# Softmax weights divided by their sums before the transposes, instead of the product after them

## The chip, the core and the metric

One core of a Trainium2 chip (trn2) runs the whole program. Its engines run side by side, each its own instructions in order: TensorE (PE in the rows, PEld for its weight loads), VectorE (DVE), ScalarE (ACT), GpSimd (POOL), and SyncE (SP), which here only issues transfers. They wait for one another by semaphores. The metric is the device time of one execution in microseconds; lower is better.

## The reference, cut to what matters

One layer of a streaming encoder, for 512 prompt frames and 64 sample frames with a cache of 128: a projection, two kinds of attention with 8 heads each, an output projection, two layer norms and a feed-forward part. The change concerns the last lines of both attentions, the softmax and the product with the values:

```
def fox_attend(q, k, v, cum_q, cum_k, q_pos, k_pos):
    s = jnp.einsum('bqhd,blhd->bhql', q, k, ...) * HEAD_DIM ** -0.5
    decay = cum_q[..., None] - cum_k[..., None, :]
    p = jax.nn.softmax(jnp.where(mask, s + decay, NEG), axis=-1)
    return jnp.einsum('bhql,blhd->bqhd', p.astype(v.dtype), v)

def dsa_attend(...):
    ...
    s = jnp.einsum('bqhd,bqkhd->bhqk', q, kg, ...) * HEAD_DIM ** -0.5
    p = jax.nn.softmax(jnp.where(valid[:, None], s, NEG), axis=-1)
    return jnp.einsum('bhqk,bqkhd->bqhd', p.astype(vg.dtype), vg)
```

`dsa_attend` keeps for each frame only the keys of the highest index scores. The division by the sum of a row may be done to the weights p, or to the product with v: both give the same result.

## The kernel before

Features lie on the partitions, the 576 frames (512 and 64) along the free axis. Products of full precision are made of three products of split numbers (a high part that ACT casts, a low part that DVE or POOL subtracts), in `gemm`, L279, 288 columns at a time. Weights come by DMA into a ring of raw buffers, ACT casts the high half (L183), DVE or POOL subtracts the low half (L187).

The heads go in eight **pairs** (p = 0 to 7): pairs 0 to 3 are the forgetting attention, 4 to 7 the indexed one. While the attention of pair p runs, the projection of pair p+1 (`proj`) runs between its steps: `drive` gives out the projection in groups of six products and puts a step of the attention between groups. Beside pair 7 runs the first part of the output projection (`wo1`).

A pair has nine **jobs**: a block of 128 query frames i = 0 to 3 for each of two heads hh (so 128, 256, 384 or 512 keys), and one job s for the 64 sample frames of both heads. A **tick** starts one job, and `PLAN` says which stage of which earlier job is due in this tick: (stage, lag) means that the stage is applied to the job started lag ticks ago. A tick has three groups of stages, with one group of projection products between two groups, and takes some 3 us. The stages of before:

- `qk`, lag 0: scores into a PSUM tile S (L825, L827; L818 for the job s)
- `addmax`, lag 1: DVE adds the bias (`causal`, `dbias`, `biasS`, `dbiasS`) and finds the row's extreme (L835), into an SBUF tile `sP`
- `exp`, lag 2: ACT takes the exponential in place (L843) and adds up each row; the sums of the eight prompt jobs go to a tile `sums` of the pair
- `norm`, lag 2: for the job s alone: DVE inverts its own sum (L848), ACT multiplies the weights (L849); then DVE inverts the pair's `sums` (L851) and ACT spreads them over 512 columns, `rows` (L853)
- `ptrans`, lag 3: PE transposes the weights in blocks of 128x128 into a PSUM tile T (the helper of all transposes is L65)
- `pevac`, lag 3: T goes to SBUF, by ACT for pairs 0 to 3 (L891), by DVE for 4 to 7 (L893)
- `scales`, lag 3: PE transposes `rows`, four blocks, into a PSUM tile X
- `pv`, lag 4: 24 products of weights and values into the PSUM tile V (L913) once a pair; two for the job s into a tile X (L902, L903)
- `oevac`, lag 5: once a pair, ACT copies the job s (L923) and the transposed sums (L924) to `mix32`, DVE multiplies V by them (L925), ACT casts the high part BH (L926), POOL subtracts the low part BL (L927).

The tiles S, T and X share one ring of three PSUM banks (tag R, `psum_1`): a fourth tile waits for the reader of the first. V has a bank of its own. The big projection tiles m have two buffers.

Beside the first pair (some 54 to 86 us) the index scores are made: PE makes a head's logits (L608), ACT takes the relu (L613) into one of four slices of `work`, DVE adds them up in `dbias` (L616, L618). They use the same three PSUM banks. Then DVE chooses the highest scores in rounds of MAX8 and MATCH_REPLACE8 (L642, L644), until some 189 us, in between its other work. Tiles named `st` hold the extremes and sums of a job and the eight maxima of a round.

The order of the instructions on each engine is fixed when the program is built.

Of the kernel before, what the change touches and what calls it, by code (L numbers as in the profile page):

```python
# [8 lines left out]
F32 = mybir.dt.float32  # L9
F32R = mybir.dt.float32r  # L10
AF = mybir.ActivationFunctionType
OP = mybir.AluOpType
# [3 lines left out]
NT = 576  # L16
NP = 512
# [19 lines left out]
def tile_hybrid_step(ctx: ExitStack, tc: tile.TileContext, I, O):  # L37
    nc = tc.nc
    PE, ACT, DVE, POOL, SP = nc.tensor, nc.scalar, nc.vector, nc.gpsimd, nc.sync
# [4 lines left out]
    def f(ap):  # L44
        return ap.bitcast(F32)
# [18 lines left out]
    def transpose(out, in_, n):  # L64
        PE.transpose(out, in_, ident[:n, :n])  # L65
# [23 lines left out]
    def drive(main, n_main, bg, n_bg, drain=True, close=True):  # L89
        done = 0  # L90
        for i, _ in enumerate(main):
            clock[0] += 1
            pop_due(POP)
            for fl in fillers:
                fl()
            while bg is not None and done * n_main < (i + 1) * n_bg:
                done += 1
                if next(bg, 0) == 0:
                    bg = None
                    break  # L100
        if close:
            flush()
        if bg is not None and drain:
            for _ in bg:
                pass
# [181 lines left out]
    sb = pA.enter_context(tc.tile_pool(name="sb", bufs=1))  # L287
# [7 lines left out]
    def psum_1(tag, bufs, dt=F32):  # L295
        return psA.tile([128, 512], dt, name=tag, tag="V" if tag == "V" else "R", bufs=1 if tag == "V" else 3)
# [369 lines left out]
    pair = {0: {}}  # L666
# [134 lines left out]
    BH = BL = None  # L801
# [27 lines left out]

    def addmax(j):  # L830
        n = j["S"].shape[1]
        t = sb.tile([128, 512], F32, name="sP", bufs=4)
        st = stats()
        j["P"], j["st"] = t[:, :n], st
        DVE.tensor_tensor_reduce(j["P"], j["S"], j["bias"], scale=1.0, scalar=-GONE, op0=OP.add, op1=OP.min,  # L835
                                 accum_out=st[:, 0:1])

    def exp(j):
        P = pair[j["p"]]
        if "sums" not in P:  # L840
            P["sums"] = sb.tile([128, 2, 4], F32, name="sums", bufs=2)
        s = j["st"][:, 2:3] if j["s"] else P["sums"][:, j["hh"], j["i"]:j["i"] + 1]
        ACT.activation(j["P"], j["P"], AF.Exp, bias=j["st"][:, 0:1], scale=-1.0, accum_out=s)  # L843

    def norm(j):

        if j["s"]:
            DVE.reciprocal(j["st"][:, 3:4], j["st"][:, 2:3])  # L848
            ACT.mul(j["P"], j["P"], j["st"][:, 3:4])  # L849
            sums = pair[j["p"]]["sums"]  # L850
            DVE.reciprocal(sums, sums)  # L851
            rows = pair[j["p"]]["rows"] = sb.tile([128, 4, 2, 64], F32, name="rows", tag="tok", bufs=2)
            ACT.copy(rows, sums.rearrange("p h (i o) -> p i h o", o=1).to_broadcast([128, 4, 2, 64]))  # L853

    def scales(j):

        if not j["s"]:
            return
        rows = pair[j["p"]]["rows"]
        ps = j["R"] = psum_1("X", 1)  # L860
        for i in range(4):
            transpose(ps[:, i * 128:i * 128 + 128], rows[:, i].rearrange("p h c -> p (h c)"), 128)

    def ptrans(j):
        ps = psum_1("T", 1)
# [50 lines left out]
    def oevac(j):  # L916
        if not j["s"]:
            return
        p = j["p"]
        mx = sb.tile([128, NT], F32, name="mix32", tag="mix32")  # L920
        for hh in range(2):
            r = slice(hh * 64, hh * 64 + 64)
            ACT.copy(mx[r, NP:], j["O"][r, r])  # L923
        ACT.copy(mx[:, :NP], j["R"])  # L924
        DVE.tensor_tensor(mx[:, :NP], pair[p]["O"], mx[:, :NP], OP.mult)  # L925
        ACT.copy(BH[:, p], mx)  # L926
        POOL.tensor_tensor(BL[:, p], mx, f(BH[:, p]), OP.subtract)  # L927

    def jobs_of(p):
        out = [dict(p=p, hh=hh, i=i, s=False, close=i % 2 == 1 and hh == 1) for i in range(4) for hh in range(2)]  # L930
        return out + [dict(p=p, s=True, close=True)]

    PLAN = (((oevac, 5), (addmax, 1), (exp, 2), (make_bias, 0), (make_bias, -1)),
            ((ptrans, 3), (norm, 2)),
            ((qk, 0), (pevac, 3), (scales, 3), (pv, 4)))

    all_jobs = [j for p in range(8) for j in jobs_of(p)]
    tick_no = [0]
# [72 lines left out]
    for p in range(7):  # L1011
        if p == 1:
# [3 lines left out]
            BH = base.tile([128, 8, NT], F32R, name="BH", tag="BH")  # L1016
# [24 lines left out]
    def wo1():  # L1041
        side = delayed(1, v_out(7))
        for j in range(8):
            u = U["o", j]
            W = WT.use(u)
            WT.ahead(u + 1)
            m = psum_m()
            for h in range(2):
                if (j, h) == (7, 1):
                    WT.ahead(u + 2)  # L1050
                for _ in gemm(m[:, h, :HW], W, range(6), BH, BL, slice(h * HW, (h + 1) * HW)):
                    WT.step()
                    if j == 0:
                        next(side, 0)
                    yield 1
                if j in (5, 6) and h == 0:
                    p_split(j - 5)
            y = Y[:, j].rearrange("p (a c) -> p a c", a=2)
            later(0, lambda y=y, m=m: DVE.scalar_tensor_tensor(
                y, y, ALPHA, m[:, :, :HW], op0=OP.mult, op1=OP.add))  # L1060

    drive(wo1(), 48, ticks(9 + 5), 42)
    pPA.close()
    pA.close()

# [488 lines left out]
```

## Time and profile before

| | |
|---|---|
| median of three runs | 781.4 us (781.35, 782.94, 781.4) |
| profiled execution | 782.97 us |
| its span, first to last instruction | 781.2 us |
| PE busy | 771.7 us, 99% |
| DVE busy | 554.7 us, 71% |
| ACT busy | 441.1 us, 56% |
| POOL busy | 118.9 us, 15% |
| TensorE clock granted | 1.000 |

Busy time is that of instructions at work; the rest of the span is waiting. In the rows of the profile a duration of a matmul is its time from issue to end, and matmuls overlap: what one costs the queue is read from the chain of waits, or from the distance between two starts. Rows of the chain and of the timeline begin with the start and the length in us; "x4" means four instructions merged in the row; what stands in brackets is the idle time before, and what ended it. Rows of the waits give the total, the number and the longest.

### The profile page before, as it was taken

To read this page: it belongs to the slowest core of one execution; us is meant where nothing else is said; L and a number is where in the kernel's file an instruction comes from. 1 tells how busy PE (TensorE), PEld (TensorE's weight loads), DVE (VectorE), ACT (ScalarE), POOL (GpSimd) and SP (SyncE) were. 2 spreads that over 40 slices of the span, in tenths; PEclk is the share of its full clock that TensorE was granted. 3 is DMA by queue.
4 is the path that set the end of the run, shared out by engine and by line. 5 is a ranking of instruction groups with operands and counts; after the bars stand their busy time and mean duration, and the time that the engine had idled before them with its cause. 6 is when DMAs were issued, how large, how long until landed. Compare 5 with 4: busy or idle time off the path is not lost.

```text
span 781.2 us, 14772 instructions
## 1 busy us (share of the span) xinstructions
PE 771.7 (99%) x5798; PEld 755.1 (97%) x5798; DVE 554.7 (71%) x1124; ACT 441.1 (56%) x924; POOL 118.9 (15%) x121
## 2 busy tenths in 40 slices
PE   9999999999999999999999999999999999999997
PEld 8988899999999999999999999999999999999997
DVE  7578787897556555989988666677666686557553
ACT  5468766788777644587366434444434454526351
POOL 8102345354332000110000000000000000022200
PEclk9999999999999999999999999999999999999999
DMA  8627233253323233441143222323222313630001
GB/s 298 204 37 173 66 113 107 88 181 115 111 65 92 73 96 112 143 164 56 55 135 108 84 79 83 109 84 105 78 63 103 110 55 112 231 130 28 28 28 67
DMA packets 31125, 81.43 MB, mean 104 GB/s; under 512 B 5072, under 2 KB 10192, under 8 KB 30928
## 3 DMA queue, kind: packets, MB, share of 16 engines
q1 hardware_dynamic: 30768, 80.27, 33.1%
q8 instruction: 45, 0.74, 0.4%
q14 instruction: 24, 0.20, 0.1%
q10 hardware_dynamic: 288, 0.22, 0.1%
HBM read 66.38 MB, written 9.54 MB: 97 GB/s over the span
## 4 chain that ended last, share of the span: by engine, by line
PE 90%; DVE 5%; ACT 2%; issue 1%; DMA 1%; POOL 0%; DVEq 0%; ACTq 0%; SPq 0%
PE g L279 54%; PE m L279 20%; PE n L279 3%; PE V L913 2%; PE T L65 2%; PE S L827 1%; PE X L65 1%; PE S L825 1%; DVE dbias L618 1%; PE m L419 1%; PE m L426 1%; PE S L426 1%; DVE whl L187 1%; DMA wraw<-in_w_up_dram 0%; DMA iraw<-in_w_idx_dram 0%
## 5 line engine op out<-in xcount | busy, mean ns | idle before, releaser
L183 ACT CAST whl<-wraw 128x512 fp32r<-128x512 f32 (+1 forms) x228 | 137.4, 611 | 179.8 <-PE g L279 150.5
L187 DVE TENSOR_TENSOR whl<-wraw,whl 128x512 fp32r<-128x512 f32 (+1 forms) x194 | 132.5, 694 | 79.0 <-ACT whl L183 78.6
L279 PE MATMUL m<-AH,whl 128*128 128x288 f32 x736 | 177.7, 308 | 0.0
L279 PE MATMUL g<-BH,whl 128*128 128x288 f32 (+2 forms) x784 | 162.9, 296 | 0.5 <-DVE Y L1219 0.5
L279 PEld LDWEIGHTS g<-BH,whl 128*128 128x128 f32 x784 | 127.7, 188 | 1.2 <-DVE Y L1219 1.0
L279 PEld LDWEIGHTS m<-AH,whl 128*128 128x128 f32 x736 | 126.3, 188 | 1.9 <-issue 1.0
L279 PE MATMUL g<-BL,whl 128*128 128x288 f32 (+2 forms) x392 | 115.5, 295 | 0.0
L279 PE MATMUL m<-AL,whl 128*128 128x288 f32 x368 | 109.0, 296 | 0.0
L279 PE MATMUL g<-hidO,whl 128*128 128x288 f32 (+2 forms) x768 | 103.8, 295 | 0.0
L279 PE MATMUL g<-hidE,whl 128*128 128x288 f32 (+2 forms) x768 | 103.7, 295 | 0.0
L279 PEld LDWEIGHTS g<-hidO,whl 128*128 128x128 f32 x768 | 102.5, 188 | 0.0
L279 PEld LDWEIGHTS g<-hidE,whl 128*128 128x128 f32 x768 | 102.2, 188 | 0.1
L279 PEld LDWEIGHTS g<-BL,whl 128*128 128x128 f32 x392 | 73.8, 188 | 0.2
L279 PE MATMUL g<-s,whl 128*128 128x288 f32 x504 | 71.3, 295 | 0.0
L279 PEld LDWEIGHTS m<-AL,whl 128*128 128x128 f32 x368 | 69.5, 189 | 0.7
L279 PEld LDWEIGHTS g<-s,whl 128*128 128x128 f32 x504 | 68.2, 188 | 0.0
L1109 POOL TENSOR_TENSOR ln_s<-Y 128x576 f32<-128x576 f32 (+2 forms) x3 | 4.4, 1468 | 374.5 <-DVE Y L1386 362.1
L187 POOL TENSOR_TENSOR whl<-wraw,whl 128x512 fp32r<-128x512 f32 x34 | 44.5, 1308 | 75.1 <-ACT whl L183 57.5
L843 ACT ACTIVATE sP<-sP,st 128x128 f32<-128x128 f32 (+4 forms) x72 | 39.6, 550 | 25.3 <-DVE st L835 24.9
L279 PE MATMUL m<-BH,whl 128*128 128x288 f32 x192 | 43.4, 304 | 0.0
L1362 DVE TENSOR_TENSOR Y<-Y,g 128x576 f32<-128x576 f32 x40 | 30.0, 749 | 14.5 <-PE g L279 14.5
L279 PEld LDWEIGHTS m<-BH,whl 128*128 128x128 f32 x192 | 32.1, 188 | 0.4 <-issue 0.3
(280 smaller groups left out, 1278.0 us busy)
## 6 DMA issues: line engine op xcount, KB each, us to landing
wraw<-in_w_up_dram SPq DMA_DIRECT2D x32, 512.0 KB, 3.5
wraw<-in_w_down_dram SPq DMA_DIRECT2D x32, 512.0 KB, 3.4
wraw<-in_w_qkv_dram SPq DMA_DIRECT2D x23, 512.0 KB, 3.8
wraw<-in_w_gate_dram SPq DMA_DIRECT2D x8, 512.0 KB, 4.0
wraw<-in_w_o_dram SPq DMA_DIRECT2D x8, 384.0 KB, 3.1
out_vT_dram<-v SPq DMA_DIRECT2D x8, 288.0 KB, 2.1
Y<-in_xT_dram SPq DMA_DIRECT2D x8, 288.0 KB, 4.7
PLD<-PL SPq DMA_DIRECT2D x4, 576.0 KB, 3.5
```

Of the source, the lines that this page charges most:

```text
L65: PE.transpose(out, in_, ident[:n, :n])
L183: ACT.copy(self.hv[h][0], src)
L187: eng.tensor_tensor(lv, src, f(hv), OP.subtract)
L279: PE.matmul(ps, W(w, kw, wc), a[:, ka, cols], start=(first and i == 0), stop=(last and i == n - 1))
L419: PE.matmul(mk[:, h, :HW], w0(part, k), a[:, k, h * HW:(h + 1) * HW], start=(k == 0 and i == 0), stop=(k == 7 and i == 2))
L426: PE.matmul(acc[b][:n[b], :304], a[:, k, b * 128:b * 128 + n[b]], ixw(part, k), start=(k == 0 and i == 0), stop=(k == 7 and i == 2))
L618: DVE.scalar_tensor_tensor(dst[:n, :nk], r[:n, :nk], w, dst[:n, :nk], op0=OP.mult, op1=OP.add)
L825: PE.matmul(ps[:, :n], Q[:, c], K[:, :n], start=True, stop=False)
L827: PE.matmul(ps[:, :n], Q[:, c], P["KL"][:, hh, :n], start=False, stop=True)
L843: ACT.activation(j["P"], j["P"], AF.Exp, bias=j["st"][:, 0:1], scale=-1.0, accum_out=s)
L913: PE.matmul(P["O"][r, (i - 1) * 128 + c.start:(i + 1) * 128], P["vt"][:, kb, r], t[:, hh, kb, c], start=(kb == 0), stop=(kb == i))
L1362: later(0, lambda y=y, m=m: DVE.tensor_tensor(y, y, m[:, :, :HW], OP.add))
```

## The change

Each job's weights are now divided by their sum, before the transposes: `norm` inverts the sum of every job on DVE (L843 of the changed file), and multiplies its weights on ACT (L845), for the first pair on POOL (L847). The pair's `sums`, `rows` and the stage `scales` are gone, and with them 32 transposes. `oevac` writes BH straight from PSUM with ACT (L910) and BL with DVE (L911), for V and for the two parts of the job s; `mix32` and POOL's subtraction are gone. `ptrans` and `pevac` have lag 4, `pv` 5, `oevac` 6, the tiles `sP` five buffers, and the attention 45 steps beside `wo1` instead of 42.

```
     def addmax(j):
-        t = sb.tile([128, 512], F32, name="sP", bufs=4)
+        t = sb.tile([128, 512], F32, name="sP", bufs=5)
...
     def exp(j):
-        P = pair[j["p"]]
-        if "sums" not in P:
-            P["sums"] = sb.tile([128, 2, 4], F32, name="sums", bufs=2)
-        s = j["st"][:, 2:3] if j["s"] else P["sums"][:, j["hh"], j["i"]:j["i"] + 1]
-        ACT.activation(j["P"], j["P"], AF.Exp, bias=j["st"][:, 0:1], scale=-1.0, accum_out=s)
+        ACT.activation(j["P"], j["P"], AF.Exp, bias=j["st"][:, 0:1], scale=-1.0, accum_out=j["st"][:, 2:3])
 
     def norm(j):
-        if j["s"]:
-            DVE.reciprocal(j["st"][:, 3:4], j["st"][:, 2:3])
+        DVE.reciprocal(j["st"][:, 3:4], j["st"][:, 2:3])
+        if j["p"]:
             ACT.mul(j["P"], j["P"], j["st"][:, 3:4])
-            sums = pair[j["p"]]["sums"]
-            DVE.reciprocal(sums, sums)
-            rows = pair[j["p"]]["rows"] = sb.tile([128, 4, 2, 64], F32, name="rows", tag="tok", bufs=2)
-            ACT.copy(rows, sums.rearrange("p h (i o) -> p i h o", o=1).to_broadcast([128, 4, 2, 64]))
-
-    def scales(j):
-        if not j["s"]:
-            return
-        rows = pair[j["p"]]["rows"]
-        ps = j["R"] = psum_1("X", 1)
-        for i in range(4):
-            transpose(ps[:, i * 128:i * 128 + 128], rows[:, i].rearrange("p h c -> p (h c)"), 128)
+        else:
+            POOL.tensor_scalar(j["P"], j["P"], j["st"][:, 3:4], None, op0=OP.mult)
...
     def oevac(j):
-        mx = sb.tile([128, NT], F32, name="mix32", tag="mix32")
+        parts = [(BH[:, p, :NP], BL[:, p, :NP], pair[p]["O"])]
         for hh in range(2):
             r = slice(hh * 64, hh * 64 + 64)
-            ACT.copy(mx[r, NP:], j["O"][r, r])
-        ACT.copy(mx[:, :NP], j["R"])
-        DVE.tensor_tensor(mx[:, :NP], pair[p]["O"], mx[:, :NP], OP.mult)
-        ACT.copy(BH[:, p], mx)
-        POOL.tensor_tensor(BL[:, p], mx, f(BH[:, p]), OP.subtract)
+            parts.append((BH[r, p, NP:], BL[r, p, NP:], j["O"][r, r]))
+        for hi, lo, ps in parts:
+            ACT.copy(hi, ps)
+            DVE.tensor_tensor(lo, ps, f(hi), OP.subtract)
...
-    PLAN = (((oevac, 5), (addmax, 1), (exp, 2), (make_bias, 0), (make_bias, -1)),
-            ((ptrans, 3), (norm, 2)),
-            ((qk, 0), (pevac, 3), (scales, 3), (pv, 4)))
+    PLAN = (((oevac, 6), (addmax, 1), (exp, 2), (make_bias, 0), (make_bias, -1)),
+            ((ptrans, 4), (norm, 2)),
+            ((qk, 0), (pevac, 4), (pv, 5)))
...
-    drive(wo1(), 48, ticks(9 + 5), 42)
+    drive(wo1(), 48, ticks(9 + 6), 45)
```

What this does to the order of the instructions, at three places.

TensorE, at the end of the first pair, where its value products stood (X of `rows` are the four transposes of the sums, V the value products):

```order
 L825 MATMUL S<-kE,qE 128x256
 L827 MATMUL S<-KLP_150,fox 128x256
-L65 MATMUL X<-ident,rows 128x128 x4
-L913 MATMUL V<-PT,vtok 64x256 x2
-L913 MATMUL V<-PT,vtok 64x128 x2
-L913 MATMUL V<-PT,vtok 64x256 x6
-L913 MATMUL V<-PT,vtok 64x128 x2
```

and one job of the next pair further on:

```order
 L825 MATMUL S<-kO,qO 128x256
 L827 MATMUL S<-KLP_150,fox 128x256
-L902 MATMUL X<-PTs,Vc 128x128
-L903 MATMUL X<-PTs,VS_157 128x128
+L898 MATMUL V<-PT,vtok 64x256 x2
+L898 MATMUL V<-PT,vtok 64x128 x2
+L898 MATMUL V<-PT,vtok 64x256 x6
+L898 MATMUL V<-PT,vtok 64x128 x2
```

The transposes of the sums have left the queue, and the value products stand one job later, where the job s had its own, which follow a job later again.

ScalarE, near the end of the index logits beside the first pair. Before:

```order
L843 ACTIVATE sP,sums<-sP,st 128x512
L613 ACTIVATE work<-S 64x192
L853 COPY rows<-sums 128x512
L613 ACTIVATE work<-X 64x192
L891 COPY PT<-T 128x3x128
L685 COPY v_1149<-m 128x576
```

and now:

```order
L839 ACTIVATE sP,st<-sP,st 128x512
L613 ACTIVATE work<-S 64x192
L613 ACTIVATE work<-X 64x192
L876 COPY PT<-T 128x3x128
L685 COPY v_1157<-m 128x576
```

The copy that spreads the sums, and that waits for DVE's inverse of them, stood between two relus of logits; nothing stands there now. The work of this pair's `norm` went to POOL, whose queue over the same stretch is now:

```order
L847 TENSOR_SCALAR sP<-sP,st 128x256 x2
L187 TENSOR_TENSOR whl<-wraw,whl 128x512
L847 TENSOR_SCALAR sP<-sP,st 128x384
L711 CAST fox<-qs 64x512
L712 CAST fox<-qs 64x512
L187 TENSOR_TENSOR whl<-wraw,whl 128x512
L847 TENSOR_SCALAR sP<-sP,st 128x384
L847 TENSOR_SCALAR sP<-sP,st 128x512
L187 TENSOR_TENSOR whl<-wraw,whl 128x512
L847 TENSOR_SCALAR sP<-sP,st 128x512
```

The multiplications (L847) are new; the casts and the weight halves between them stood there before.

VectorE, beside pair 3, between the additions of the bias of its last prompt job and of its job s. Before:

```order
L835 ISA sP,st<-S,causal 128x512
L835 ISA st 128x1
L728 TENSOR_TENSOR qE<-x_2248,qE 64x576
L729 TENSOR_TENSOR qO<-x_2248,qO 64x576
L642 MAX st<-dbias_99 128x8
L851 RECIPROCAL sums<-sums 128x8
L644 MATCH_REPLACE dbias_99<-st,dbias_99 128x512
L642 MAX st<-dbias_99 128x8
L835 ISA sP,st<-S,biasS 128x192
```

and now:

```order
L835 ISA sP,st<-S,causal 128x512
L835 ISA st 128x1
L728 TENSOR_TENSOR qE<-x_2269,qE 64x576
L729 TENSOR_TENSOR qO<-x_2269,qO 64x576
L642 MAX st<-dbias_99 128x8
L843 RECIPROCAL st<-st 128x1 x2
L644 MATCH_REPLACE dbias_99<-st,dbias_99 128x512
L642 MAX st<-dbias_99 128x8
L835 ISA sP,st<-S,biasS 128x192
```

The rounds of the choice stand as they did; the inverse of the pair's sums has become the inverses of two single jobs, each behind ACT's exponential of its job.

## The prediction, made before the changed kernel ran

> **What bounds the kernel now.** First the page: busy time of each engine, then the busy time of stretches, one a pair or more.
>
> ```profile
> PE 771.7 (99%) x5798; PEld 755.1 (97%) x5798; DVE 554.7 (71%) x1124; ACT 441.1 (56%) x924; POOL 118.9 (15%) x121
> 66.00:94.00 28.00, 26.41 (x186) 24.16 (x184) 23.36 (x59) 21.29 (x60) 8.97 (x8) 1.00 0.44 129
> 122.40:150.75 28.35, 28.35 (x224) 27.26 (x225) 22.53 (x65) 19.45 (x51) 14.16 (x13) 1.00 0.37 108
> 150.75:179.10 28.35, 28.35 (x223) 27.22 (x224) 25.20 (x63) 24.01 (x58) 13.59 (x11) 1.00 0.52 163
> 179.10:207.40 28.30, 28.30 (x224) 27.21 (x223) 18.22 (x57) 22.75 (x53) 11.79 (x9) 1.00 0.30 97
> 345.00:700.00 355.00, 355.00 (x2697) 354.95 (x2696) 259.70 (x434) 171.20 (x289) 2.59 (x2) 1.00 0.31 100
> ```
>
> The columns of a stretch are its length, then PE, PEld, DVE, ACT and POOL busy with their instructions, the clock and the DMA share. TensorE is busy without a gap in the middle pairs, and from 345 to 700 us, behind the attention: what leaves its queue there shortens the run, as long as nothing it waits for gets late. Only beside the first pair does it miss 1.59 us of 28. The waits say for whom:
>
> ```profile
> PE X L608 <- ACT work L613: 1.4, 2, 1.2
> PE g L279 <- DVE Y L1219: 0.5, 1, 0.5
> ```
>
> So the first pair is bound by ACT and DVE, which make the index logits, and the rest by TensorE. Beside pair 3 (the fourth row) DVE is at 89% and ACT at 85%: that is where added work could show.
>
> **The change: what leaves TensorE.** The chain of waits gives the pace, here of the end of the first pair:
>
> ```profile
> 93.52 0.12 PE S L827
> 93.64 0.44 PE X L65 x4
> 94.08 2.31 PE V L913 x24
> ```
>
> ```profile
> L65 PE MATMUL X<-ident,rows 128*128 128x128 f32 x32 | 4.8, 272 | 0.0
> ```
>
> Four transposes hold the queue for 0.44 us, 0.11 each; 32 of them make 3.5 us. The value products (2.31 us a pair), the transposes of the weights and those of the job s stay, a tick later; the step of the plan adds no product. By the group's mean of 272 ns they would make 8.7 us; but that is the time from issue to end of one that overlaps its neighbours, and the queue moved on after 0.11. I take 3.5 us. The Trainium skill (TensorE: Matmul & The Clock Gate, Part 4: PE-mode transpose) gives about 275 ns for such a transpose inside a kernel, so it would come to some 8.8 us; the 272 ns agree with its figure, the 0.44 us for four don't agree with that use of it.
>
> **What is added to ACT and DVE in pairs 1 to 7.** These rows price it:
>
> ```profile
> L843 ACT ACTIVATE sP<-sP,st 128x512 f32<-128x512 f32 x16 | 11.5, 719 | 7.7 <-DVE st L835 7.6
> L843 ACT ACTIVATE sP<-sP,st 128x384 f32<-128x384 f32 x16 | 9.9, 616 | 6.3 <-DVE st L835 6.2
> L843 ACT ACTIVATE sP<-sP,st 128x256 f32<-128x256 f32 x16 | 8.2, 510 | 0.2
> L843 ACT ACTIVATE sP<-sP,st 128x128 f32<-128x128 f32 x16 | 6.4, 401 | 10.5 <-DVE st L835 10.5
> L849 ACT ACTIVATE sP<-sP,st 128x192 f32<-128x192 f32 x8 | 3.7, 457 | 0.2 <-DVE st L848 0.2
> L853 ACT COPY rows<-sums 128x512 f32<-128x512 f32 x8 | 4.9, 614 | 0.9 <-DVE sums L851 0.9
> L926 ACT CAST BH<-mix 128x576 fp32r<-128x576 f32 x8 | 5.4, 669 | 0.1
> L848 DVE RECIPROCAL st<-st 128x1 f32<-128x1 f32 x8 | 1.3, 161 | 1.1 <-ACT sP L843 0.9
> L851 DVE RECIPROCAL sums<-sums 128x8 f32<-128x8 f32 x8 | 1.6, 198 | 2.2 <-ACT sP L843 2.1
> ```
>
> The multiplication of the job s took as long as its exponential (0.457 us), so the eight others get the exponentials' durations: 2 x (0.401 + 0.510 + 0.616 + 0.719) = 4.5 us of ACT a pair. `rows` (0.614) and the cast of `mix32` (0.669) go; the copy of the transposed sums becomes the cast of V, 512 columns either way. ACT gains some 3.2 us a pair. DVE gains eight inverses of 0.161 less one of 0.198, 1.1 us; its multiplication by the sums becomes the subtraction of V, the same size; two subtractions of 64x64 are new, which no row shows. Bounded by the inverse of a single column (0.161) and by the addition of the bias over 192 columns (0.34, in a row below), they get 0.2 each, near the smaller one. DVE gains 1.5 us a pair, POOL loses a subtraction.
>
> What covers this? The weights must be divided before their transposes, and these come a tick later, some 3 us. In the tightest place that I looked at:
>
> ```profile
> 158.48 0.51 ACT L843 ACTIVATE sP<-sP,st 128x256 f32<-128x256 f32 x1
> 162.09 0.38 PE L65 MATMUL T<-ident,sP 128*128 128x128 f32 x2
> ```
>
> the exponential was done 3.1 us before its transposes; one tick more makes it 6 us, and inverse plus multiplication need 0.161 + 0.510 and two hand-overs. So the transposes themselves won't wait. The other cover is the ring of three PSUM banks. Its margin is the time between a bank's release and the next use of it. With the transposed sums gone, which held a bank until `oevac`, it grows; the smallest that I found elsewhere is beside pair 3:
>
> ```profile
> 158.52 0.56 DVE L835 CUSTOM_DVE_ANT_0 sP<-S,causal 128x384 f32<-128x384 f32 x1 [0.60 <-PE S L827]
> 169.48 0.49 PE L818 MATMUL S<-KcT,QB 128*128 128x192 f32 x2
> 172.33 0.34 DVE L835 CUSTOM_DVE_ANT_0 sP<-S,biasS 128x192 f32<-128x192 f32 x1
> 172.83 0.62 PE L65 MATMUL X<-ident,v 128*128 128x128 f32 x4
> ```
>
> The scores of the job s (169.48) wait 2.4 us for DVE, which reads them until 172.67; the third tile after them, X at 172.83, needs their bank: 0.16 us of margin. DVE didn't rest since 158.52, so all that is added in between makes it late. That is four inverses more for one less (0.64 - 0.2) and the two small subtractions (0.4): 0.85 us, so TensorE waits some 0.7 us there. Bounds: nothing, if DVE's gap before 158.52 takes it up; 3.0 us, if ACT can use none of its idle time for its 3.2 us (less the margin): then it drags along DVE's inverses, which wait for its exponentials and stand in DVE's queue before the additions of the bias, and TensorE waits for those. I take 0.7, as DVE's own rows give it.
>
> **The first pair.** Here the multiplication is POOL's, and nine inverses join DVE in the stretch that is bound by the logits.
>
> ```profile
> 82.89 0.19 DVE L851 RECIPROCAL sums<-sums 128x8 f32<-128x8 f32 x1
> 83.11 0.62 ACT L853 COPY rows<-sums 128x512 f32<-128x512 f32 x1 [0.88 <-DVE sums L851]
> 83.64 0.32 ACT L613 ACTIVATE work<-X 64x192 f32<-64x192 f32 x1
> 84.01 0.30 PE L608 MATMUL X<-Z 128*64 128x192 f32 x1 [1.20 <-ACT work L613]
> ```
>
> Reading upwards: TensorE's one long wait (1.20 us) is for a relu that stood behind `rows`, which stood idle for DVE's inverse. All of that goes, so 1.2 us can be won. Against it stands DVE's delay. Jobs 2 to 5 have their inverses between two gaps of DVE, at 60.27 and at 77.82 us, which hide those before and the next one: 4 x 0.161 = 0.6 us. And POOL's multiplications meet DVE's additions of logits:
>
> ```profile
> 60.27 0.48 DVE L618 SCALAR_TENSOR_TENSOR dbias<-work,iw,dbias 128x256 f32<-128x256 f32 x1 [0.86 <-ACT work L613]
> ...
> 69.53 1.40 POOL L187 TENSOR_TENSOR whl<-wraw,whl 128x512 fp32r<-128x512 f32 x1 [3.24 <-issue]
> 69.93 2.41 DVE L618 SCALAR_TENSOR_TENSOR dbias<-work,iw,dbias 128x512 f32<-128x512 f32 x2
> 71.86 0.95 POOL L711 CAST fox<-qs 64x512 fp32r<-64x512 f32 x1 [0.92 <-ACT qs L704]
> 72.87 0.61 POOL L712 CAST fox<-qs 64x512 fp32r<-64x512 f32 x1
> 76.38 0.74 DVE L618 SCALAR_TENSOR_TENSOR dbias<-work,iw,dbias 128x512 f32<-128x512 f32 x1
> 77.82 0.75 DVE L618 SCALAR_TENSOR_TENSOR dbias<-work,iw,dbias 128x512 f32<-128x512 f32 x1 [0.70 <-ACT work L613]
> ```
>
> Two additions took 2.41 us where one alone takes 0.74: 0.9 us lost while POOL's subtraction ran, and nothing visible from the cast at 71.86, which itself took 0.95 instead of 0.61. No row shows POOL's multiplication. By the cast it takes 0.61 us for 512 columns, by the subtraction 1.40; jobs 2 to 7 have 2304 columns, so 2.7 to 6.3 us of POOL. DVE's loss lies between nothing (the cast's) and all 6.3. With one input it is nearest to the cast: I take 0.9. The first pair comes to 0.6 + 0.9 - 1.2 = +0.3 us, bounded by -0.6 and +5.7.
>
> The Trainium skill (SBUF — State Buffer, Who interferes with whom) says that a VectorE instruction with two SBUF inputs and a GpSimd one that reads SBUF exclude each other for a whole instruction, whichever starts first. That speaks against this change, and the 2.41 us agree with it; it is the first rival below.
>
> **The end.** TensorE's waits name neither POOL's subtraction (L927) nor the copies before it, so a shorter way from V to BH and BL wins nothing. The 0.5 us at L1219 may go or double: nothing in the sum.
>
> **The sum.** -3.5 + 0.7 + 0.3 = -2.5 us. The profiled execution took 782.97 us (span 781.2), so it would take 780.5; the median of the runs stands 1.6 lower, 781.4, and becomes 778.9.
>
> **The rivals.**
>
> 1. POOL blocks DVE beside the first pair. For: the 2.41 us. Against: the cast cost DVE nothing. If each blocks DVE fully: 781.4 - 3.5 + 0.7 + 5.7 = 784.3, slower. It takes the whole gain from a loss of some 3.4 us on DVE on, about half of its upper end.
> 2. Both engines get late beside pair 3: the transposes' gain becomes a wait for the ring. For: DVE 25.2 + 1.5 and ACT 24.0 + 3.2 of 28 us, each waiting for the other in order. Against: in the next pair DVE has 10 us to spare. With 3.0 us instead of 0.7: 781.2, no change.
> 3. The waits stay away and only the gains count: -3.5 - 0.6 us, 777.3.
> 4. A transpose costs its 272 ns: 781.4 - 8.7 + 1.0 = 773.7. Against it is the chain.
>
> **Chances.** The forecast 0.55, rival 1 0.12, rival 2 0.25, rival 3 0.07, rival 4 0.01. A measurement here can tell some 0.2%, 1.6 us, from no change (the three runs differ by as much). The forecast and rivals 3 and 4 are faster: 0.63. Rival 2 is no change: 0.25. Rival 1 is slower: 0.12. The range reaches from rival 3 with half a microsecond at the end (776.8) to past rival 2, into a part of rival 1: 782.6.
>
> **What would show it.** Right: no X of `rows`, some 0.44 us less from one pair's value products to the next, TensorE without a wait from 90 to 150 us, and less than 1.4 us waiting for L613. Wrong: additions L618 that again take twice their 0.74 us beside POOL's multiplications (rival 1); a wait of TensorE between 165 and 190 us for L835 or for a multiplication on ACT of more than 1 us (rival 2).

## The result, and the profile after

The changed kernel took 777.56 us (median; 777.53 to 777.63), the kernel before 781.38: a ratio of 0.9947, with a 95% interval of 0.9937 to 0.9957, so 3.8 us less. The prediction said 2.5 us less (778.9), and the time is inside its range. The executions of a kernel fall into two groups some 1.5 us apart, which part in the first 10 us (last section), so all times that follow are medians of the lower groups, and distances in the traces are taken from a mark behind that start. Of the 5.4 us between the spans of the two profiles (781.2 and 775.8), 1.6 lie ahead of that mark.

The page of the changed kernel:

```profile
PE 765.7 (99%) x5766; PEld 749.7 (97%) x5766; DVE 563.3 (73%) x1196; ACT 459.0 (59%) x963; POOL 119.5 (15%) x122
```

32 instructions left TensorE; ACT and DVE grew by 18 and 9 us. The chain of waits of the changed kernel, at three pairs' value products (start, us, engine, tile, line):

```profile
92.31 2.31 PE V L898 x24
...
120.21 2.31 PE V L898 x24
...
148.10 2.31 PE V L898 x24
```

From one to the next it is 27.90 and 27.89 us. Before it was 28.33 and 28.34 (starts at 94.08, 122.41 and 150.75, with four X of `rows` ahead of each): 0.44 us less a pair, 3.5 us in eight pairs. That is the sum's first term as it stood.

What is left are waits. TensorE's, in the changed kernel:

```profile
PE X L65 <- DVE st L835: 1.0, 1, 1.0
...
PE n L1137 <- DVE ln_s L1130: 0.5, 1, 0.5
...
PE S L608 <- DVE st L835: 0.3, 1, 0.3
PE X L65 <- ACT v L685: 0.3, 1, 0.3
PE g L279 <- DVE Y L1203: 0.2, 1, 0.2
PE X L608 <- ACT work L613: 0.2, 1, 0.2
```

The 1.4 us for the relus of the logits (L613) fell to 0.2; 1.0 us is new beside pair 3. To see how much TensorE rests in each place, take the busy time of the stretches from the transposes of one pair's v to the next pair's (length; PE, PEld, DVE, ACT, POOL busy), the first pair's without its first 3.6 us, in which TensorE has no rest. The kernel before stands first, then the changed one; in each, the first pair is above and pair 3 below:

```profile
58.63:87.83 29.20, 27.44 (x186) 24.88 (x185) 24.34 (x56) 24.46 (x66) 8.32 (x8) 1.00 0.56 128
144.51:172.83 28.32, 28.32 (x223) 27.19 (x222) 24.13 (x59) 23.33 (x55) 13.19 (x11) 1.00 0.39 130
```

```profile
57.06:84.25 27.19, 26.51 (x183) 24.36 (x181) 24.70 (x60) 23.07 (x62) 18.50 (x15) 1.00 0.59 137
140.03:169.12 29.09, 28.06 (x219) 26.79 (x218) 25.79 (x70) 25.62 (x60) 11.04 (x10) 1.00 0.41 133
```

TensorE rested 29.20 - 27.44 = 1.76 us beside the first pair and now rests 0.68: 1.08 won, where the prediction had 0.3 lost. Beside pair 3 it rested nothing and now rests 1.03; the prediction had 0.7. So the account is -3.52 - 1.08 + 1.03 = -3.57 us. Its terms hold to some 0.2 us: the stretch of pair 5 takes 28.11 us, 0.22 more than the 27.89 of an undisturbed pair, without an idle row. Another 0.2 us lie behind the attention (from the first product into a tile `g`, with which that part begins, to the end of the span it takes 474.06 us before and 473.83 now).

### The profile page after: what moved, and what is told of

The parts are those of the page before. It is cut to its first block, busy times and chain, and to the rows that moved or that the text cites. A ratio compares the mean times of both kernels' runs of the same rounds, so it can differ in the third digit from the quotient of the medians.

```text
span 775.8 us, 14798 instructions
## 1 busy us (share of the span) xinstructions
PE 765.7 (99%) x5766; PEld 749.7 (97%) x5766; DVE 563.3 (73%) x1196; ACT 459.0 (59%) x963; POOL 119.5 (15%) x122
## 4 chain that ended last, share of the span: by engine, by line
PE 89%; DVE 6%; ACT 2%; issue 1%; DMA 1%; POOL 0%; SPq 0%; DVEq 0%; ACTq 0%
PE g L279 54%; PE m L279 20%; PE n L279 3%; PE V L898 2%; PE T L65 2%; PE S L827 1%; PE S L825 1%; DVE dbias L618 1%; PE m L419 1%; PE m L426 1%; PE S L426 1%; ACT whl L183 1%; PE X L65 1%; DVE whl L187 1%; DVE Y L1203 1%
## 5 line engine op out<-in xcount | busy, mean ns | idle before, releaser
L187 DVE TENSOR_TENSOR whl<-wraw,whl 128x512 fp32r<-128x512 f32 (+1 forms) x194 | 132.0, 692 | 69.6 <-ACT whl L183 69.3
L187 POOL TENSOR_TENSOR whl<-wraw,whl 128x512 fp32r<-128x512 f32 x34 | 44.7, 1314 | 73.6 <-ACT whl L183 49.7
L839 ACT ACTIVATE sP<-sP,st 128x128 f32<-128x128 f32 (+4 forms) x72 | 39.5, 550 | 14.2 <-DVE st L835 13.8
L845 ACT ACTIVATE sP<-sP,st 128x128 f32<-128x128 f32 (+4 forms) x63 | 34.2, 549 | 5.1 <-DVE st L843 4.3
```

Source lines behind the costliest of these rows:

```text
L187: eng.tensor_tensor(lv, src, f(hv), OP.subtract)
```

## The experiments

"From the mark" means from the first transposes of `kstack` (35.72 us before, 34.16 us after), which lie behind the start.

| kernel | us | against the changed kernel |
|---|---|---|
| the kernel before | 781.38 | +3.8 |
| the changed kernel | 777.55 | |
| 32 transposes put back | 780.16 | +2.6 |
| before, without `rows` and its transposes | 776.33 | -1.2 |
| first pair not divided | 777.74 | +0.2 |
| first pair's multiplications on ACT | 779.82 | +2.3 |
| ticks as before | 780.58 | +3.0 |
| every inverse twice | 778.52 | +1.0 |
| pair 3's multiplications on POOL | 776.70 | -0.9 |
| top-k rounds spread thinner | 778.01 | +0.5 |
| multiplications of pairs 0, 3, 6 on POOL | 776.18 | -1.4 |
| all multiplications on POOL | 775.89 | -1.7 |

### What the transposes cost

Four transposes of a constant tile for each pair are put back into the changed kernel; nothing reads them.

```diff
+    def dummy(j):
+        if not j["s"]:
+            return
+        ps = psum_1("X", 1)
+        for i in range(4):
+            transpose(ps[:, i * 128:i * 128 + 128], ones, 128)
...
-            ((qk, 0), (pevac, 4), (pv, 5)))
+            ((qk, 0), (pevac, 4), (dummy, 4), (pv, 5)))
```

> The changed kernel with four transposes of a constant tile put back for each pair, 32 in all, ahead of the value products; nothing reads them. Theory Q (the gain is the queue time of TensorE; what the change wins in waits beside the first pair, 1.1 us, it gives back beside pair 3, 1.0 us): from the first product of the projections of pair 0 on, the two traces differ by 3.8 us of TensorE's busy time, 0.12 us a transpose, so this kernel takes 777.6 + 3.8 = 781.4 us, 781.0 to 781.8, and the distance between the value products of two middle pairs is 28.33 us again. Rival L (a transpose costs the 272 ns of its group's row): 777.6 + 8.7 = 786.3. Rival W (the gain came from waits that went with the reads of the transposed sums, on ACT and DVE): 777.6 to 778.5, since no wait comes back.

Measured: 780.16 us, between W's range and Q's. The chain of this kernel, at the same two pairs:

```profile
92.33 0.43 PE X L65 x4
92.76 2.31 PE V L905 x24
...
120.66 0.43 PE X L65 x4
121.09 2.32 PE V L905 x24
```

Q's unit price was wrong and the prediction's right: the distance is 28.33 us again, 0.44 more than without, 0.11 a transpose and not 0.12 (the whole 3.8 us by 32). L (8.7 us) and W (at most 1) are out. The missing 0.9 us are lost in the changed kernel and not here: beside pair 3 TensorE waits 0.33 us instead of 1.03, and the stretch of pair 5, which has no idle row in either, takes 28.33 us for 28.11, only 0.22 more. 3.52 - 0.70 - 0.22 = 2.60, and from the mark to the first product `g` it takes 270.43 us for 267.81, 2.62 more. So the transposes are worth 3.5 us, and the wait beside pair 3 hangs on how the work there happens to fall.

### What the removal alone would have brought

The kernel before, without `rows`, their inverse and transposes:

```diff
-            sums = pair[j["p"]]["sums"]
-            DVE.reciprocal(sums, sums)
-            rows = pair[j["p"]]["rows"] = sb.tile([128, 4, 2, 64], F32, name="rows", tag="tok", bufs=2)
-            ACT.copy(rows, sums.rearrange("p h (i o) -> p i h o", o=1).to_broadcast([128, 4, 2, 64]))
...
-        ACT.copy(mx[:, :NP], j["R"])
+        ACT.copy(mx[:, :NP], pair[p]["O"])
```

> The kernel before without the spread sums (rows), their inverse and their 32 transposes; nothing else is added. The sums are not used: the copy ahead of the multiplication of V takes V itself, so that ACT and DVE do an instruction of the same size there. Theory Q: the 32 transposes are worth 3.8 us and the wait for the relu behind rows 1.2 us, nothing is added beside pair 3: 781.4 - 5.0 = 776.4, 776.0 to 776.8. Rival W2 (the relu is late for the logits' own sake, and rows only stood at that place): the wait of TensorE at L613 stays over 0.8 us and the time is 777.4 to 777.8.

Measured: 776.33 us, as Q had it. This kernel leaves out the division of the prompt frames' products altogether. The wait at L613 falls to 0.2 us, so it did come from `rows` in ACT's queue, and W2 falls. With 781.38 - 776.33 = 5.05 us for the removal, all that the change adds costs 777.55 - 776.33 = 1.2 us net, and the wait beside pair 3, which this kernel doesn't have, is 1.03 us.

### The first pair

What the change adds there is left out:

```diff
     def norm(j):
-
+        if not j["p"]:
+            return
         DVE.reciprocal(j["st"][:, 3:4], j["st"][:, 2:3])
```

> The changed kernel without the inverses and multiplications of the first pair: its weights stay undivided. This prices what the change adds there. By the prediction's two terms (0.6 us for four inverses of DVE, 0.9 us for POOL meeting DVE's additions): 777.55 - 1.5 = 776.05, and pair 1 begins 1.5 us earlier. By the waits that are left in the changed kernel's first pair (0.19 us for the relu, 0.33 us for an addition of DVE): 0.2 to 0.5 us earlier, 777.1 to 777.4, if the wait beside pair 3 stays as it is.

Measured: 777.74 us, no gain at all: pair 1's v comes 50.23 us from the mark, in the changed kernel 50.09. The prediction's 1.5 us aren't there, nor are the 0.2 to 0.5 us that the waits promised. DVE's additions of logits in this stretch show why (the groups of 512 columns and of the new positions: before, in the changed kernel, and in this one, without the multiplications):

```profile
L618 DVE SCALAR_TENSOR_TENSOR dbias<-work,iw,dbias 128x512 f32<-128x512 f32 x7 | 6.9, 984 | 1.1 <-ACT work L613 0.7
...
L618 DVE SCALAR_TENSOR_TENSOR dbiasS<-work,iw,dbiasS 64x192 f32<-64x192 f32 x7 | 3.8, 539 | 1.7 <-ACT work L613 1.5
```

```profile
L618 DVE SCALAR_TENSOR_TENSOR dbias<-work,iw,dbias 128x512 f32<-128x512 f32 x7 | 7.0, 997 | 0.7 <-ACT work L613 0.6
...
L618 DVE SCALAR_TENSOR_TENSOR dbiasS<-work,iw,dbiasS 64x192 f32<-64x192 f32 x7 | 4.5, 644 | 0.8 <-ACT whl L183 0.5
```

```profile
L618 DVE SCALAR_TENSOR_TENSOR dbias<-work,iw,dbias 128x512 f32<-128x512 f32 x7 | 7.0, 1002 | 0.9 <-ACT work L613 0.7
...
L618 DVE SCALAR_TENSOR_TENSOR dbiasS<-work,iw,dbiasS 64x192 f32<-64x192 f32 x7 | 4.6, 652 | 0.7
```

They did get longer than before, by 0.1 and 0.7 us here, but without POOL's multiplications they are just as long. All sizes together take 16.5 us before, 17.5 in the changed kernel and 17.4 without the multiplications, so of the 0.9 us expected of POOL's multiplications some 0.1 is left. Without them, the additions of 1.2 us and more all ran beside POOL's subtractions for the weights (L187). POOL is the one that lost: its nine multiplications take 11.8 us here, and 9.4 by their undisturbed times (last section). DVE waited less for relus in exchange for the longer additions (0.7 + 1.5 us, now 0.6 and nothing that is named; all rest ahead of these rows fell from 2.8 to 1.5), and it still rests 27.19 - 24.70 = 2.5 us in the stretch. The inverses were charged to the end, although DVE had rest to pay them from.

The same multiplications on ACT:

```diff
-        if j["p"]:
+        if True:
             ACT.mul(j["P"], j["P"], j["st"][:, 3:4])
```

> The changed kernel with the multiplications of the first pair on ACT instead of POOL. Theory P (POOL is the cheap place there: its multiplications hold up neither ACT nor DVE): ACT is busy 23.1 of 27.2 us beside the first pair and gets nine multiplications, 4.95 us, so the relus of the logits get late and TensorE waits for them: 1 to 3 us more, 779.5 us, 778.6 to 780.6. Rival A (ACT has room, since what it waits for is DVE and not its own queue): 777.3 to 777.9. Rival D (POOL holds up DVE's additions by its port, so ACT is the better place): below 777.2.

Measured: 779.82 us; P holds. TensorE's waits in this kernel's first pair:

```profile
71.22 0.44 PE L825 MATMUL S<-kO,qO 128*128 128x384 f32 x1 [1.17 <-ACT work L613]
83.57 0.30 PE L608 MATMUL X<-Z 128*64 128x192 f32 x1 [1.25 <-ACT work L613]
```

Pair 1 begins 3.0 us later (53.07 us from the mark), and 0.7 of it come back beside pair 3, where the wait is 0.35 us. The place of the work decided this stretch, not its amount: nine multiplications of together 5.0 us on ACT, on whose relus TensorE depends, cost 3 us, and on POOL, where they take 11.8 us, nothing.

### What the extra tick hides

```diff
-    PLAN = (((oevac, 6), (addmax, 1), (exp, 2), (make_bias, 0), (make_bias, -1)),
-            ((ptrans, 4), (norm, 2)),
-            ((qk, 0), (pevac, 4), (pv, 5)))
+    PLAN = (((oevac, 5), (addmax, 1), (exp, 2), (make_bias, 0), (make_bias, -1)),
+            ((ptrans, 3), (norm, 2)),
+            ((qk, 0), (pevac, 3), (pv, 4)))
...
-    drive(wo1(), 48, ticks(9 + 6), 45)
+    drive(wo1(), 48, ticks(9 + 5), 42)
```

(and four weight tiles `sP` instead of five)

> The changed kernel with the steps at the ticks of the kernel before (transposes and their copies 3, value products 4, last step 5, four weight tiles instead of five). Theory T (the extra tick is needed by POOL's multiplications of the first pair, up to 1.7 us each with 1.4 us of weight subtractions ahead in POOL's queue, and hardly by ACT's): TensorE waits beside the first pair for sP of the multiplication 2 to 4 us in all, less than 0.5 us in pairs 1 to 7 beyond what it waits now: 780.5 us, 779.5 to 782. Rival N (the tick hides nothing that was not hidden by the 3.1 us before): 777.3 to 778.0. Rival E (each pair waits, since ACT's multiplication comes behind two exponentials): 0.5 us and more a pair, over 782.

Measured: 780.58 us. The time is T's, the places aren't, and N and E are out. TensorE's waits in the pairs 3 and 4 of this kernel:

```profile
169.83 0.66 PE L65 MATMUL T<-ident,sP 128*128 128x128 f32 x4 [1.82 <-ACT sP L845]
191.92 0.55 PE L65 MATMUL T<-ident,sP 128*128 128x128 f32 x3 [0.34 <-ACT sP L845]
198.42 0.66 PE L65 MATMUL T<-ident,sP 128*128 128x128 f32 x4 [0.68 <-ACT sP L845]
```

The stretches of the pairs 3 and 4 take 0.9 and 1.6 us more; the first pair takes 1.2 more, with 0.7 us of waiting for POOL. So the tick is needed by ACT's multiplications too, beside the pairs 3 and 4, and without it (and without the fifth tile, which went with it) the change would bring 0.8 us instead of 3.8.

### Who makes the wait beside pair 3

The prediction put it on DVE's own additions. Every inverse done twice tests that:

```diff
         DVE.reciprocal(j["st"][:, 3:4], j["st"][:, 2:3])
+        DVE.reciprocal(j["st"][:, 3:4], j["st"][:, 2:3])
```

> The changed kernel with every inverse done twice on DVE, 72 more of 0.157 us. Theory D: three of them stand between DVE's last rest before the wait of pair 3 and the addition of the job s, so that wait grows from 1.03 to about 1.5 us, and elsewhere they are hidden: 778.0 us, 777.8 to 778.5. Rival A (ACT sets that wait): the wait stays within 0.2 us, 777.4 to 777.7. Rival F (DVE is the bound beside the first pair, as the prediction had it with its 0.6 us for four inverses): another 0.6 us there, 778.6 or above.

Measured: 778.52 us, more by TensorE's waits at two other places and not there:

```profile
PE X L65 <- ACT v L685: 1.6, 2, 0.8
...
PE X L65 <- DVE st L843: 0.8, 1, 0.8
```

Beside pair 3 it is 0.85 us, less than in the changed kernel and within A's 0.2. What is new are two waits of 0.8 us, beside the pairs 4 and 6, for ACT's copy of v, where the changed kernel has one of 0.3. F falls (pair 1 begins no later), and the wait that D was made for didn't grow; the time is D's by other waits. Against D this is no clean test, though: between the added inverses DVE rests 0.32 us at 160.27 us for ACT, its rest for the cast BH is 0.11 us instead of 0.40, and L724 (below) takes 0.97 us instead of 1.16. Why ACT's copy of v gets late was not tested; ACT's multiplications wait for the inverses and stand in the same queue.

The other side: the multiplications of pair 3 on POOL as well.

```diff
-        if j["p"]:
+        if j["p"] not in (0, 3):
             ACT.mul(j["P"], j["P"], j["st"][:, 3:4])
```

> The changed kernel with the multiplications of pair 3 on POOL too. Theory D: ACT's time doesn't matter beside pair 3, DVE's queue stays as it is, and POOL's 1.7 us a multiplication are inside the 6 us that the transposes leave: the wait stays 0.8 to 1.3 us, 777.3 to 777.9. Rival A: with 4.5 us less on ACT the wait goes: 776.4 to 776.8. Rival L (POOL's reads hold up DVE's additions of two tiles in SBUF, of which the rotation there has seven for each projection of 0.75 us): DVE's rows of 0.75 us get to 1 us and more in the mean, the wait grows over 2 us, 778.5 or above.

Measured: 776.70 us and no wait beside pair 3: rival A. TensorE's transposes of v there, in the changed kernel, and then in this one:

```profile
169.12 0.63 PE L65 MATMUL X<-ident,v 128*128 128x128 f32 x4 [1.03 <-DVE st L835]
```

```profile
167.93 0.60 PE L65 MATMUL X<-ident,v 128*128 128x128 f32 x4
```

DVE's time line there (start, us, line, operation, tile), in the changed kernel, and then in this one:

```profile
156.05 0.23 DVE L911 TENSOR_TENSOR BL<-X,BH 64x64 fp32r<-64x64 f32 x1 [0.40 <-ACT BH L910]
...
162.32 1.16 DVE L724 TENSOR_TENSOR x<-x,xr 128x576 f32<-128x576 f32 x1
...
168.63 0.34 DVE L835 CUSTOM_DVE_ANT_0 sP<-S,biasS 128x192 f32<-128x192 f32 x1
```

```profile
155.62 0.23 DVE L911 TENSOR_TENSOR BL<-X,BH 64x64 fp32r<-64x64 f32 x1
...
161.88 0.74 DVE L724 TENSOR_TENSOR x<-x,xr 128x576 f32<-128x576 f32 x1
...
167.84 0.34 DVE L835 CUSTOM_DVE_ANT_0 sP<-S,biasS 128x192 f32<-128x192 f32 x1
```

And ACT's and POOL's time lines in the changed kernel:

```profile
153.92 0.51 ACT L845 ACTIVATE sP<-sP,st 128x256 f32<-128x256 f32 x1
154.34 0.23 ACT L742 COPY KcT<-x 128x64 f32<-128x64 f32 x1
154.47 0.20 ACT L910 CAST BH<-X 64x64 fp32r<-64x64 f32 x1
154.57 0.61 ACT L839 ACTIVATE sP<-sP,st 128x384 f32<-128x384 f32 x1
...
155.19 0.60 ACT L183 CAST whl<-wraw 128x512 fp32r<-128x512 f32 x1
155.81 0.21 ACT L910 CAST BH<-X 64x64 fp32r<-64x64 f32 x1
```

```profile
162.26 0.61 POOL L747 CAST KLP<-zero 32x512 fp32r<-32x512 f32 x1
```

In the changed kernel DVE is 0.43 us later from the subtraction at 156.05 on, since it rested 0.40 us for ACT's second small cast to BH, which came at 155.81, behind a multiplication (153.92), an exponential and a cast of weights. It loses another 0.42 us at L724, which takes 1.16 us instead of 0.74 while POOL runs a cast that began 0.06 us ahead of it. Together that is some 0.8 us: the scores of the job s are read until 168.97 instead of 168.18, and TensorE, which comes for their bank at 168.09, waits 1.03. The first part is ACT's queue, the second is what POOL happens to do at that moment.

Two more things can be read from the traces. With 0.8 us less, TensorE would still have to wait 0.1 to 0.25 us for those scores, but in this kernel X starts at 167.93, before they are read to the end at 168.18. So here X doesn't wait for that bank; which bank it has instead, and why, is not shown. And two of the kernels above, with the transposes put back and with the first pair's multiplications on ACT, leave pair 3's multiplications on ACT, while L724 takes its 0.75 and 0.74 us and DVE rests 0.22 and 0.26 us for the cast BH: their waits beside pair 3 are 0.33 and 0.35 us. So about two thirds of the 1.03 us go with the meeting at L724 and half of that rest. What ACT's queue alone would leave was not tried.

The third try leaves the multiplications and inverses where they are and puts off top-k rounds, from pair 1 on:

```diff
         if p == 1:
+            state["rate"] = 0.55
             while not state["logits"]:
```

> The changed kernel with the rounds of the top-k spread thinner from pair 1 on: 0.55 us of them per step of the projections instead of 0.63, so that they end some 14 us later, beside pair 4, where DVE has more room. Theory D (the 1.03 us wait of TensorE beside pair 3 is DVE's queue: the rounds stand among its inverses and additions): a seventh fewer rounds between DVE's last rest and the addition for the job s, some 1.2 us, so the wait goes or falls under 0.3 us: 776.6 us, 776.4 to 776.9. Rival A (the wait is made by ACT's multiplications, on whose hand-overs DVE's inverses depend): the wait stays 0.8 to 1.2 us, 777.3 to 777.8. Rival M (the rounds that are put off are forced together at the additions of pair 4): a new wait of TensorE in pair 4 of 1 us or more, 777.6 or above.

Measured: 778.01 us: the time is rival M's. The wait for the scores' bank beside pair 3 is gone, as D had it (L724 takes 0.74 us here), and another of 0.34 us stands near it, for ACT's copy of T. The stretch of pair 4 takes 29.34 us for 27.92, with idle rows of 0.58 and 0.15 us for DVE. Put off, the rounds cost more there than they cost here.

### A version that is faster than both

The first pair and pair 3 both say that POOL is the cheap place for the multiplications. First the pairs 0, 3 and 6, then all (`if j["p"] not in (0, 3, 6):` and `if False:` in the place of `if j["p"]:`).

> The changed kernel with the multiplications of the pairs 0, 3 and 6 on POOL. Beside pair 6 TensorE waits 0.31 us for ACT's copy of v. Theory A (ACT's queue is what the multiplications lengthen): that wait goes too, 776.4 us, 776.2 to 776.5, against 776.7 with pairs 0 and 3. Rival S (that wait was 0.25 us in the kernel before and isn't made by the multiplications): 776.6 to 776.8. Rival L (POOL's queue makes the low halves of the weights late, which TensorE then waits for): 777 or above.

> The changed kernel with all multiplications on POOL. One took 0.60, 0.91, 1.23 and 1.56 us for 128 to 512 columns beside pair 3 where nothing met it, and 0.76 for the job s: 9.4 us a pair, so POOL goes from some 12 to 21.5 of 27.9 us. Theory A: with ACT's queue free, and 6 us ahead of the transposes, no wait of TensorE is left in the pairs: 776.3 to 776.8. Rival L (POOL and DVE exclude each other where DVE has two inputs in SBUF, and the low halves of weights stand in POOL's queue behind the multiplications): TensorE waits for sP of POOL or for whl, 777.5 or above.

Measured for the first: 776.18 us, with the wait for v gone (A, at the edge of its range), a ratio to the kernel before of 0.9933, interval 0.9920 to 0.9947. With all on POOL it is 775.89 us in two of five executions, and 777.33 to 777.52 in the other three (ratio over all 0.9936, 0.9924 to 0.9949). That is A by its waits, no wait of TensorE for sP or weights is left in the pairs, and the time is 0.4 us below A's range. The page of the second:

```profile
PE 767.5 (99%) x5766; PEld 751.8 (97%) x5766; DVE 565.1 (73%) x1196; ACT 430.4 (55%) x900; POOL 188.7 (24%) x185
```

POOL takes 69 us more, ACT 29 less. The 0.3 us between the two versions stand in the traces as well (266.46 and 266.18 us from the mark to the first `g`).

## Why the prediction was right, and where it wasn't

- **The transposes.** -3.5 us by the pace of the chain; 0.44 us a pair came out, with and without the rest of the change. The 272 ns of the group's row are no price in a queue: 32 transposes put back cost 3.5 us before waits, not 8.7. The 275 ns of the Trainium skill (TensorE: Matmul & The Clock Gate, Part 4: PE-mode transpose) agree with the row's time from issue to end; taken as a cost in this queue they are 2.5 times too high.
- **What ACT and DVE get.** The estimates from neighbours held: multiplications of 401 to 723 ns (estimated 401 to 719), inverses 157, subtractions of 64x64 219 (200).
- **The wait beside pair 3.** The place and the ring of three banks (the scores of the job s, X of v behind them) were right, and 0.7 us was 1.03. The reason given, DVE's own rows, was not enough: with these rows in place and pair 3's multiplications on POOL the scores are read at 168.18 us, at most 0.25 us after TensorE comes. The rest is DVE's 0.40 us of waiting for ACT's cast and the 0.42 us at L724, neither of them in the sum, so that 0.7 came near is partly luck. The prediction's own sign of rival 2, a wait of more than 1 us for L835 between 165 and 190 us, did appear. But its mechanism, DVE dragged by ACT, made about 0.4 us of it, where rival 2 had put 3.0.
- **The first pair.** This is the term that was mis-sized: +0.3 us was predicted and -1.08 measured. The gain of 1.2 us from the relu behind `rows` came as said. The 0.6 us of inverses were charged in full to the end, and cost nothing: DVE had 4.9 us of rest in that stretch and keeps 2.5. The 0.9 us of meeting POOL hardly came: the additions take 17.5 us with the multiplications and 17.4 without. POOL's multiplications of the jobs 2 to 7 took 9.0 us (1.13, 1.68 and 1.67 us for 256, 384 and 512 columns), past the upper bound of 6.3, and that cost nothing either.
- **Rival 1** (POOL blocks DVE) showed its sign, additions L618 of up to 1.33 us instead of 0.74, but the kernel without the multiplications has additions of 1.2 us and more as well. The multiplications cost these additions some 0.1 us in all, far from the 3.4 us from which this rival decides.
- **Rival 3** (777.3, all waits stay away) came nearest in time, nearer than the forecast's 778.9, but not by its mechanism: the wait beside pair 3 is there, and the first pair and the end won more than it had.
- **The end.** Nothing was in the sum; 0.2 us were won behind the attention. The traces narrow it down: the kernel before without `rows` still takes 474.06 us there, as the kernel before does, and the changed kernel takes 473.84 with the transposes put back, 473.86 with the old ticks and 473.85 with all multiplications on POOL. So the gain belongs neither to the transposes nor to the tick; the new `oevac` and the inverses remain, and which of them wins it stays open.
- **The extra tick** was described as cover; together with the fifth weight tile it is worth 3.0 us.

## What to carry to other kernels

Work moved off a saturated engine is worth its pace in that engine's queue, read from the chain, not the duration of one instruction. Work added to another engine can be paid from that engine's rest, as beside the first pair, so count the rest before charging anything. But the rest must lie between the added work and the instruction that others wait for: beside pair 3 DVE had 28.32 - 24.13 = 4.2 us of rest before, and TensorE still lost 1.03. Where two engines hand work to each other in order, look for the instruction that stands behind the added one in its queue. An idle engine that is twice as slow, as POOL is here, can be the cheapest place, if nothing waits for it.

## What the hardware showed unexpectedly

**TensorE's start.** In the upper group the first products run at little more than half their pace. Rows of TensorE's time line, before (upper) and after (lower):

```profile
9.73 0.46 PE L426 MATMUL m<-iw,AH 128*128 128x304 f32 x1
9.99 0.46 PE L426 MATMUL m<-iw,AL 128*128 128x304 f32 x1
```

```profile
8.57 0.30 PE L426 MATMUL m<-iw,AH 128*128 128x304 f32 x1
8.71 0.30 PE L426 MATMUL m<-iw,AL 128*128 128x304 f32 x1
```

They start 0.25 us apart until 10.5 us, there 0.14 us from 5.5 us on; the granted clock of the stretches is 1.00 in both. From then on the two are alike: of all profiles here the mark is at 35.7 us in three and at 34.2 in the others, the three being the profiled executions of the upper group. The kernel before was in it in 10 of 47 executions. The Trainium skill (TensorE: Matmul & The Clock Gate, Part 1: The HAM clock gate) tells of a clock that doubles after a busy window which runs freely, so that the moment varies from run to run; the two paces agree with that, but no run here shows the window itself, nor why there are just two groups.

The changed kernel was run again, and with 11 instead of 8 products on a constant tile ahead of everything (`WARM = 11`), to fill the rest before the first real ones:

> The changed kernel itself once more, beside the others on the same chip, to see how its executions spread: the kernel before and four variants so far had two groups of times 1.5 us apart, the six executions of this one had one. If TensorE's pace in the first 10 us decides the group by chance, as the two traces look, 1 to 5 of some 10 executions stand at 779.1 us and the others at 777.5; if the change itself removes the upper group, all stand at 777.5.

> The changed kernel with 11 instead of 8 products on a constant tile at the very start, which fills the 0.44 us that TensorE rests at 4.8 us; the 0.7 us that it adds lie ahead of a wait of 0.9 us for AL. Theory G (the upper group of times, some 1.5 us above the lower one, is made by TensorE at half its pace until about 10 us, and the rest at 4.8 us decides): no execution in the upper group, all at 777.5 to 777.7. Rival C (chance that these products don't touch): about a quarter of the executions at 779.1, as for the kernels so far.

Measured: four from 777.52 to 777.66 us and one at 779.11, so the change doesn't remove the upper group; with 11 products all five from 777.54 to 777.59. The five of the kernel with doubled inverses have no upper group either, with 8 products, so five are too few: G is neither shown nor excluded.

**POOL beside DVE.** One multiplication by a column on POOL, of the same size, beside pair 3 in the kernel with that pair on POOL:

```profile
157.75 1.23 POOL L847 TENSOR_SCALAR sP<-sP,st 128x384 f32<-128x384 f32 x1
...
161.87 1.86 POOL L847 TENSOR_SCALAR sP<-sP,st 128x384 f32<-128x384 f32 x1
```

The first ran beside the top-k rounds and additions that read PSUM; the second met the rotation's addition L724 (161.88, 0.74 us), which has two inputs in SBUF, and took 0.63 us more. In the changed kernel it was L724 that took 0.42 us more, with POOL's cast ahead of it by 0.06 us. Four other kernels show the same pair. With the doubled inverses the cast is 0.24 us ahead, and L724 takes 0.22 us more. In three others L724 is ahead by 0.12 to 0.23 us (transposes put back, first pair on ACT, rounds spread thinner): L724 takes its 0.74 or 0.75 us, and the cast 1.06, 1.10 and 0.98 us instead of 0.61. So in these five the one that comes second pays. The multiplication at 161.87 starts too near to L724 to say which was first. The Trainium skill (SBUF — State Buffer, Who interferes with whom) tells of such an exclusion between a VectorE instruction with two SBUF inputs and a GpSimd one that reads SBUF, decided by the order of issue; these traces agree. Undisturbed, POOL took 0.60, 0.91, 1.23 and 1.56 us for 128 to 512 columns, 2.2 times ACT's 0.72 at 512.
